# FFN norm of a hybrid decoder step: transposes by the DMA crossbar in place of TensorE and PSUM

## The chip, the cores and the metric

One Trainium2 chip, all eight cores, batch split over the cores, one launch. The metric is the device time of the slowest core in microseconds (us). Some executions fall in a second, slower state, in which the cores of a die run at a lower granted TensorE clock (in one run on record, of before_held, 1143.48 us with one die at clocks of 0.80 to 0.83, where fast runs of the same kernel took 1017 to 1026 us at 0.95 to 0.97). A run is also called slow when it is over 1.5% above the fastest of its kernel. Medians below are of all runs of a kernel, slow ones too.

## The reference

One layer: an RMS norm, one wide input projection, two groups of mixer heads (a gMLP and an mLSTM), an output projection with residual; then the part that the change touches, an RMS norm and a squared-ReLU MLP; then a gated per-layer embedding (PLE).

```python
D_MODEL = 1024; BATCH = 8; SEQ = 2048; DEC_BATCH = 128; DEC_SEQ = 8; D_FF = 4 * D_MODEL
def _layer(h, pe, state, ...):
    ...                                           # mixer: norm, projections, gMLP, mLSTM with carried state C, n, m
    h = h + jnp.concatenate([y_gm, y_ml], axis=-1) @ w_out
    # channel mixer: squared-ReLU MLP
    f = rmsnorm(h, norm_ffn) @ w_up
    h = h + jnp.square(jax.nn.relu(f)) @ w_down
    # per-layer input embedding
    gate = jax.nn.sigmoid(rmsnorm(h, norm_ple) @ w_ple_gate)
    h = h + gate * (pe @ w_ple_proj)
    return h, state, vg
```

Per core this is one prompt sequence of 2048 tokens (16 tiles of 128) and 16 sample sequences of 8 tokens (one more tile). The samples carry an mLSTM state, `state_C` (`sC` below), which is loaded from memory.

## The kernel before

The 17 tiles run in two super-groups: first eight prompt tiles and the sample tile, then eight prompt tiles. Each goes through a mixer stage (A), an MLP stage (B) and a PLE stage (C). The MLP streams its weights in four quarters, and takes tiles in groups of three. At the end of each mixer stage there is a *hand-over*, where the FFN norm of the first tiles must be done before TensorE can begin on the MLP. The change acts at the two hand-overs, nine tiles at the first, eight at the second.

The norm of a tile, with its transposes:

```python
def norm_T(g, so, hsrc, abf, dst, goff, junk=None):
    ss, rs, tmp = small(g, so, 1), small(g, so + 1, 1), small(g, so + 2, 1)
    act(abf if junk is None else junk, hsrc, AF.Square, accum=ss)      # ScalarE; its by-product goes into abf too
    rstd(rs, tmp, ss, 1.0 / DM, EPS)                                   # GpSimd
    o_ = act(abf, hsrc, AF.Copy, scale=rs)                             # ScalarE: fp32 -> bf16
    p = psb("N")                                                       # one PSUM bank
    trs([(p[:, kc * 128:(kc + 1) * 128], abf[:, kc * 128:(kc + 1) * 128], IDB[:]) for kc in range(8)])   # TensorE
    tt("dve", dst, p.rearrange("p (k t) -> p k t", k=8),
       GN[:, goff:goff + 8].unsqueeze(2).to_broadcast([128, 8, 128]), ALU.mult)   # VectorE: the gain
    return o_
```

The MLP stage around it. `AB` has two buffers; the weight loads, which cast fp32 to bf16, go through GpSimd's queue (q0 below):

```python
def load_q(qd):                                   # one quarter of w_up and of w_down
    ...
    for hf in range(2):
        dma(wu[:, :, hf * 512:(hf + 1) * 512], w_up_v[:, :, c0:c0 + 512], eng="pool")
    for hf in range(2):
        dma(wd[:, hf * 4:(hf + 1) * 4, :], w_down[r0:r0 + 512, :].rearrange("(f p) n -> p f n", p=128), eng="pool")
...
load_q(0)
for i, t in enumerate(sg):
    sl = t["slot"]
    norm_T(sl, 44, H[:, sl, :], AB[i % 2], A2T[sl // 3][:, :, sl % 3 * 128:(sl % 3 + 1) * 128], G_FFN)
load_q(1)
tgs = [sg[0:3], sg[3:6], sg[6:]]
for qd in range(4):
    for tg in tgs:
        ffn_group(qd, tg)                         # 64 matmuls of 128x384, then 48 of 128x512
        ...                                       # stage C after the last quarter
    ...
    if qd == 1:
        dma(WG, w_pg.rearrange("(k p) n -> p k n", p=128), eng="pool")   # PLE weights
        ...
    if qd + 2 < 4:
        load_q(qd + 2)
```

At the end of the last mixer tile the prompt state is stored, through SyncE's queue:

```python
if t["i"] == NPT - 1:
    for h in range(4):
        dma(o_Cp[h], CST[:, h, 0:128])                                                        # 4 x 64 KB
    dma(o_Np.rearrange("h d -> d h"), CST[:, :, 128], allow_slow_non_contiguous=True)         # 2 KB
    dma(o_Mp.rearrange("a h -> h a"), MPREV[:, 0:1], allow_slow_non_contiguous=True)
```

None of this is run in the order written. A list scheduler puts the operations of each engine in a fixed order at build time, from a model of their cost. In that model all DMAs, whoever issues them, share one pipe:

```python
if o.dma:
    free[e] = s + o.cost
    d0 = max(free[e] + 1.0, dma_free)
    dma_free = d0 + o.nbytes / 290e3
    o.fin = dma_free + 1.2
```

## Time and profile before

The median of the first three runs is 1023.42 us (1022.73 to 1027.23). The profiled execution spans 1020.3 us on its slowest core, core 2; the eight cores span 1003.6 to 1020.3 us, at granted clocks of 0.950 to 0.959.

| reading | before |
|---|---|
| TensorE busy | 895.8 us, 88% |
| chain that ended last | 75% TensorE, 9% DMA, 6% VectorE |
| TensorE busy in the first hand-over, 190-235 us | 23.5 of 45 us |
| TensorE busy in the middle of the second MLP, 760-935 us | 174.3 of 175 us |

All operations are emitted by one helper, so all have line L252 (DMA issues L276). One reads by the names of the tiles: `AR` is the big SBUF arena, `pb` a PSUM bank, `IDB` the identity, `GN` the gains, `H` the residual. The page of before, from its parts on busy time, queues, chain and groups (a group gives: operation and shape, count | busy us, mean ns of one | idle us of the engine just before them, what ended most of it):

```profile
PE 895.8 (88%) x5807; PEld 539.0 (53%) x5875; DVE 581.2 (57%) x1118; ACT 391.8 (38%) x711; POOL 264.4 (26%) x370
...
q0 software_dynamic: 54224, 59.18, 40.9%
q1 hardware_dynamic: 26380, 30.32, 9.8%
...
PE 75%; DMA 9%; DVE 6%; issue 5%; ACT 3%; POOL 2%; DVEq 0%; SPq 0%; POOLq 0%; ACTq 0%
...
L252 PE MATMUL pb<-AR 128*128 128x512 bf16 (+4 forms) x4856 | 838.0, 331 | 62.3 <-DVE AR L252 20.9
...
L252 ACT ACTIVATE AR<-H 128x1024 bf16<-128x1024 f32 x68 | 71.7, 1054 | 54.4 <-PE pb L252 26.9
L252 PE MATMUL pb<-IDB,AR 128*128 128x128 bf16 x578 | 53.5, 237 | 42.6 <-ACT AR L252 28.7
...
L252 DVE TENSOR_TENSOR AR<-pb,GN 128x1024 bf16<-128x1024 bf16 x51 | 61.6, 1218 | 36.4 <-PE pb L252 36.4
```

Two DMA queues: q0, the weights, and q1, which holds everything that SyncE issues (packets, MB, share of 16 engines' span). The `IDB` group holds all the transposes; 136 of the 578 belong to the FFN norm. The multiply by a gain takes 1.22 us.

The waits of TensorE in before (what it waited for: total us, times, longest):

```profile
PE pb L252 <- DVE AR L252: 29.6, 31, 3.2
PE pb L252 <- DMA AR<-sC: 15.7, 1, 15.7
```

TensorE in time order in before (start us, us, operation, count, [idle before it <- what ended it]), around the first and the second hand-over:

```profile
218.80 1.03 PE L252 MATMUL pb<-AR 128*128 128x129 bf16 x8 [15.66 <-DMA AR<-sC]
...
232.10 2.05 PE L252 MATMUL pb<-IDB,AR 128*128 128x128 bf16 x16 [3.81 <-ACT AR L252]
234.69 4.59 PE L252 MATMUL pb<-AR 128*128 128x384 bf16 x16 [0.54 <-DVE AR L252]
...
725.94 3.21 PE L252 MATMUL pb<-AR 128*128 128x384 bf16 x24 [0.31 <-DVE AR L252]
```

Three things are to be seen. Sixteen transposes, two tiles' worth, take 2.05 us. The first up-projections of the MLP, `128x384`, start almost without a wait. And they start while the mixer is not finished: after 234.69 and after 725.94 mixer matmuls still follow, so the MLP fills the mixer's gaps. The large wait at the first hand-over is for the sample state, `sC`.

The windows of before (stretch, then length and busy us of PE, PEld, DVE, ACT and POOL with counts, then granted clock, DMA share, GB/s):

```profile
195.00:270.00 75.00, 48.20 (x330) 30.85 (x332) 39.56 (x86) 25.26 (x49) 24.42 (x33) 0.77 0.80 112
760.00:935.00 175.00, 174.32 (x1009) 98.77 (x1018) 74.86 (x127) 38.75 (x81) 8.06 (x12) 1.00 0.49 79
```

### The profile page before, as it was taken

What the parts mean: (1) busy time and instruction counts of PE and PEld (TensorE: products, weight loads), DVE (VectorE), ACT (ScalarE), POOL (GpSimd) and SP (SyncE); (2) the same over time, 40 slices, a digit from 0 to 9 for tenths busy, and PEclk for the clock granted to TensorE, in tenths of its full rate; (3) what the DMA queues carried; (4) which work ended last, traced back from release to release, by engine and by line L of the source; (5) the groups of instructions that cost most, each with busy time, mean ns of one, the idle gap of its engine ahead of it and who ended that gap; (6) DMA issues with size and microseconds to landing.
All of it is one profiled execution on the core that took longest, in us unless ns stands there. A gap on an engine that the chain in (4) does not pass through costs nothing.

```text
span 1020.3 us, 17111 instructions; the slowest of 8 cores (1003.6 to 1020.3 us)
## 1 busy us (share of the span) xinstructions
PE 895.8 (88%) x5807; PEld 539.0 (53%) x5875; DVE 581.2 (57%) x1118; ACT 391.8 (38%) x711; POOL 264.4 (26%) x370
## 2 busy tenths in 40 slices
PE   2578898937999999999997678998899999999994
PEld 2465476624455555555553267576656555565542
DVE  2354878445656774444665537988864444445664
ACT  4245356425311121114544547655532112124543
POOL 3233345443202220011232323545520001001211
PEclk9798899967999999999999889999999999999997
DMA  9993010996677768065249400003999909000111
GB/s 166 183 172 45 12 45 6 109 146 97 104 142 136 177 161 133 1 86 88 86 105 203 121 22 2 1 2 51 138 144 162 161 2 155 11 1 4 68 45 62
DMA packets 80689, 90.59 MB, mean 89 GB/s; under 512 B 13656, under 2 KB 62044, under 8 KB 80604
## 3 DMA queue, kind: packets, MB, share of 16 engines
q0 software_dynamic: 54224, 59.18, 40.9%
q1 hardware_dynamic: 26380, 30.32, 9.8%
q8 instruction: 48, 0.79, 0.3%
q14 instruction: 37, 0.30, 0.1%
HBM read 134.74 MB, written 13.93 MB: 146 GB/s over the span
## 4 chain that ended last, share of the span: by engine, by line
PE 75%; DMA 9%; DVE 6%; issue 5%; ACT 3%; POOL 2%; DVEq 0%; SPq 0%; POOLq 0%; ACTq 0%
PE pb L252 75%; DVE AR L252 3%; DMA AR<-sC 3%; DMA AR<-w_in 3%; DMA AR<-pp 2%; ACT AR L252 2%; POOL SMALL L252 1%; DMA H<-xp 1%; DVE H L252 1%; DVE SMALL L252 1%; DVE ROWX L252 1%; ACT L252 1%; POOL AR L252 0%; DVE ROWR L252 0%; POOL CST L252 0%
## 5 line engine op out<-in xcount | busy, mean ns | idle before, releaser
L252 PE MATMUL pb<-AR 128*128 128x512 bf16 (+4 forms) x4856 | 838.0, 331 | 62.3 <-DVE AR L252 20.9
L252 PEld LDWEIGHTS pb<-AR 128*128 128x128 bf16 x4924 | 470.8, 100 | 393.8 <-issue 86.3
L252 ACT ACTIVATE AR<-pb 128x384 f32<-128x384 f32 (+5 forms) x349 | 175.5, 513 | 476.0 <-PE pb L252 387.7
L252 DVE TENSOR_TENSOR H<-H,pb 128x512 f32<-128x512 f32 x170 | 116.4, 685 | 136.5 <-PE pb L252 136.3
L252 DVE TENSOR_TENSOR AR<-AR 128x384 bf16<-128x384 f32 (+2 forms) x209 | 122.8, 589 | 109.1 <-ACT AR L252 108.3
L252 ACT ACTIVATE AR<-H 128x1024 bf16<-128x1024 f32 x68 | 71.7, 1054 | 54.4 <-PE pb L252 26.9
L252 PE MATMUL pb<-IDB,AR 128*128 128x128 bf16 x578 | 53.5, 237 | 42.6 <-ACT AR L252 28.7
L252 POOL TENSOR_SCALAR SMALL<-SMALL 128x1 f32<-128x1 f32 x85 | 26.3, 310 | 245.4 <-ACT AR L252 201.9
L252 DVE TENSOR_TENSOR AR<-pb,GN 128x1024 bf16<-128x1024 bf16 x51 | 61.6, 1218 | 36.4 <-PE pb L252 36.4
L252 POOL TENSOR_TENSOR SMALL<-SMALL,NEGH 128x1 f32<-128x1 f32 (+1 forms) x102 | 69.3, 681 | 49.8 <-DVE SMALL L252 29.6
L252 PEld LDWEIGHTS pb<-IDB,AR 128*128 128x128 bf16 x578 | 43.0, 107 | 57.7 <-issue 48.9
L252 ACT ACTIVATE AR<-H,SMALL 128x1024 bf16<-128x1024 f32 x51 | 58.1, 1145 | 35.3 <-POOL SMALL L252 34.9
L276 POOL DMA_DIRECT2D AR<-w_up x16 | 15.0, 935 | 132.7 <-PE pb L252 132.3
L252 DVE TENSOR_TENSOR AR<-pb,AR 128x512 f32<-128x512 f32 (+3 forms) x86 | 43.7, 523 | 9.4 <-ACT AR L252 8.4
L252 ACT ACT_TABLE_LOAD x29 | 37.2, 1283 | 16.1 <-PE pb L252 10.2
L252 DVE SCALAR_TENSOR_TENSOR AR<-AR,pb 128x512 f32<-128x512 f32 x34 | 23.2, 684 | 29.6 <-PE pb L252 20.8
L252 ACT ACTIVATE AR<-AR 128x512 f32<-128x512 f32 x34 | 21.3, 629 | 23.8 <-DVE AR L252 17.2
L252 POOL TENSOR_TENSOR AR<-AR,GROW 128x512 bf16<-128x512 f32 (+1 forms) x19 | 25.5, 1341 | 16.5 <-PE pb L252 8.5
L276 POOL DMA_DIRECT2D AR<-w_in x12 | 11.0, 920 | 68.3 <-PE pb L252 64.3
L252 DVE SCALAR_TENSOR_TENSOR AR<-H,SMALL,AR 128x1024 f32<-128x1024 f32 x17 | 22.9, 1346 | 9.1 <-POOL SMALL L252 8.7
L252 ACT ACTIVATE AR<-pb,GSM 128x129 f32<-128x129 f32 x68 | 20.7, 366 | 13.7 <-PE pb L252 13.5
L276 POOL DMA_DIRECT2D AR<-w_down x16 | 12.2, 765 | 51.4 <-PE pb L252 51.3
(101 smaller groups left out, 434.7 us busy)
## 6 DMA issues: line engine op xcount, KB each, us to landing
AR<-w_up POOLq DMA_DIRECT2D x16, 1024.0 KB, 16.0
AR<-w_down POOLq DMA_DIRECT2D x16, 1024.0 KB, 18.9
AR<-w_in POOLq DMA_DIRECT2D x12, 1024.0 KB, 17.5
H<-xp SPq DMA_DIRECT2D x16, 512.0 KB, 4.6
y_p<-AR SPq DMA_DIRECT2D x16, 512.0 KB, 2.9
AR<-w_out POOLq DMA_DIRECT2D x2, 2048.0 KB, 41.8
AR<-sC SPq DMA_DIRECT2D x8, 512.0 KB, 5.0
AR<-w_pg POOLq DMA_DIRECT2D x2, 2048.0 KB, 27.4
```

Source lines behind the costliest of these rows:

```text
L252: ins = getattr(e, name)(**kw)
L276: lambda e, out=out, in_=in_, sem=sem, kw=kw: e.dma_start(out=out, in_=in_, **kw).then_inc(sem, 16))
```

## The change

The intent is to take the FFN norm's transposes off TensorE, the busiest engine, and to free a PSUM bank: SyncE issues one transposing DMA per tile (128x1024 bf16, 256 KB, SBUF to SBUF), and VectorE then multiplies in place.

```diff
+        def dma_t(out, in_):
+            nb = 2 * _nelem(out) * 128
+            return P.add("sp", (out, in_, dict(transpose=True)), [in_], [out], 0.06, dma=True, nbytes=nb)
+
-        def norm_T(g, so, hsrc, abf, dst, goff, junk=None):
+        def norm_T(g, so, hsrc, abf, dst, goff, junk=None, xbar=False):
             ss, rs, tmp = small(g, so, 1), small(g, so + 1, 1), small(g, so + 2, 1)
             act(abf if junk is None else junk, hsrc, AF.Square, accum=ss)
             rstd(rs, tmp, ss, 1.0 / DM, EPS)
             o_ = act(abf, hsrc, AF.Copy, scale=rs)
+            if xbar:
+                dma_t(dst, abf)
+                tt("dve", dst, dst, GN[:, goff:goff + 8].unsqueeze(2).to_broadcast([128, 8, 128]), ALU.mult)
+                return o_
             p = psb("N")
@@ stage B
-                norm_T(sl, 44, H[:, sl, :], AB[i % 2], A2T[sl // 3][...], G_FFN)
+                norm_T(sl, 44, H[:, sl, :], AB[i % 2], A2T[sl // 3][...], G_FFN, xbar=True)
```

The other two norms keep their TensorE transposes.

More of the change, by code (lines that the diff above doesn't have):

```diff
@@ L1222, in build @@
                 sl = t["slot"]
-                norm_T(sl, 44, H[:, sl, :], AB[i % 2], A2T[sl // 3][:, :, sl % 3 * 128:(sl % 3 + 1) * 128], G_FFN)
+                norm_T(sl, 44, H[:, sl, :], AB[i % 2], A2T[sl // 3][:, :, sl % 3 * 128:(sl % 3 + 1) * 128], G_FFN, xbar=True)
             load_q(1)
```

## The prediction

> **What bounds the kernel now.** TensorE. The page gives PE 88% busy and 75% of the chain that ended last. In the middle of the MLP it is packed: the window view gives PE 174.3 of 175 us at 760-935. It is not where the mixer hands over to the MLP: PE 23.5 of 45 us at 190-235, 56.3 of 60 at 700-760. The change acts only there (nine tiles, then eight).
>
> **What goes.** Per tile eight 128x128 PE transposes and one PSUM bank. The PE timeline shows 16 of them in 2.05 us, so about 1.0 us per tile, 17 us in all. That bounds the gain.
>
> **What stays.** The VectorE gain multiply (1.22 us from PSUM). It now reads bf16 from SBUF[...]: I expect 1.1-1.25 us.
>
> **What comes.** 17 SyncE DMAs of 256 KB, SBUF to SBUF. [...] the trace of before has none of the first, and its TensorE transposes take about 130 ns each, pipelined. [...] weights load at the hand-overs. DMA share is about 1.1 at 190-240 and at 705-780. There SyncE's own DMAs of 64-512 KB took 8 to 20 us to land (64 KB state stores 9.1-14.3, a 512 KB load 19.9), against 3.7 us for 512 KB in a quiet stretch. Estimate for a transpose: 4-5 us quiet, 10-18 us (central 13) beside weight loads.
>
> **Critical path.** Two AB buffers feed the transposes. TensorE let AB go within 1 us; now it is held until the DMA lands, and the square of tile i+2 writes into AB too. So tiles go in pairs: landing + about 4-5 us (square 1.24, rstd on POOL 1.3, scale 1.15, twice over ScalarE). The first MLP group needs tiles 0-2, so two rounds. The static order also moves: the first up-projection goes behind all, or most, of the last mixer stage, where before it filled that stage's gaps.
>
> - Second hand-over: before starts the first group at 725.9 and has it done at 757.6. After: norms of tiles 2 and 3 stand behind the mixer's ScalarE work, about 738; transposes issue about 742, land about 755, multiply, group starts about 757 and needs 22 us of PE: done about 779. Loss about 21 us, of which about 8 is not the DMA.
> - First hand-over: two transposes can run in the 15.7 us wait for the state load, but they share its DMA. Group start 234.7 -> about 247, partly paid back by mixer work done earlier and by absent transposes: loss about 4 us.
> - Idle TensorE restarts at a low clock (granted 0.50 at 210-220 in the window view): 1-2 us.
>
> Later groups have 22 us of PE work to hide two tiles' transposes; that holds below about 17 us of landing.
>
> **Time.** 1023.4 + about 25 = **1048 us**, 8 in 10 within 1025-1078. Faster by over 2%: 0.03; within 2%: 0.40; slower by over 2%: 0.57.
>
> **What shows it.** PE busy down 15-18 us, yet a longer span; new idle of TensorE before the 128x384 matmuls at both hand-overs, ended by the VectorE multiply behind a DMA; transposes landing in 10 us or more at the second; the multiply near 1.2 us; squares on ScalarE waiting on a DMA; the rest of the MLP unchanged.
>
> **What would make it wrong.** Landings near 4 us even beside weight loads: then about +10 us. Transposes that crowd out weight loads, or land after 20 us: 1070 and more. Mixer stage ending sooner without interleaved MLP work: a smaller loss.

"The first" are transposes by DMA, and the two landing estimates are from the landings of before that stand in front of them. The sum came to 21 + 4 = 25 us on top of 1023.4 (the 1-2 us for the clock stand outside it). The low clock of an idle TensorE is in the traces: in before 0.50 was granted in 210-220 us, where TensorE was busy for 1.2 of 10 us, and 1.00 in 240-250; in after it was 0.50 in 806-809 us, right behind a hole of 35.3 us, and 1.00 in 810-815.

## The result, and the profile after

The result is correct. The median is 1095.38 us (1093.41 to 1098.69, 4 runs) against 1024.8 us for before in the same rounds: ratio 1.0691, 95% interval 1.0651 to 1.0731, slower. Ratios here and below are the mean time of one kernel's fast runs over that of the other's of the same rounds, so not quite the ratio of the medians that are quoted. The direction was predicted. The size was not: +71 us against +25.

The page of after, the lines that answer to those of before:

```profile
PE 902.1 (83%) x5739; PEld 534.0 (49%) x5739; DVE 587.1 (54%) x1118; ACT 392.2 (36%) x711; POOL 269.1 (25%) x370
...
q0 software_dynamic: 54224, 59.18, 40.7%
q1 hardware_dynamic: 44332, 34.78, 13.8%
...
PE 65%; DMA 20%; DVE 5%; issue 4%; ACT 3%; POOL 2%; SPq 1%; DVEq 0%; POOLq 0%; ACTq 0%
...
L252 PE MATMUL pb<-AR 128*128 128x512 bf16 (+4 forms) x4924 | 852.7, 334 | 131.9 <-DVE AR L252 64.5
...
L252 ACT ACTIVATE AR<-H 128x1024 bf16<-128x1024 f32 x68 | 71.7, 1055 | 99.2 <-DMA AR<-AR 61.7
...
L252 PE MATMUL pb<-IDB,AR 128*128 128x128 bf16 x442 | 42.8, 238 | 38.1 <-ACT AR L252 25.7
...
L252 DVE TENSOR_TENSOR AR<-AR,GN 128x1024 bf16<-128x1024 bf16 x17 | 20.4, 1219 | 49.9 <-DMA AR<-AR 49.9
```

The transposes left TensorE as intended: 136 fewer, 10.7 us less busy. The in-place multiply takes 1219 ns, the same as from PSUM. The hardware queue has 17,952 more packets, which is 1,056 for each of 17 transposes, for only 4.46 MB. DMA's share of the chain rose from 9% to 20%.

The waits of TensorE in after:

```profile
PE pb L252 <- DVE AR L252: 70.7, 28, 35.3
PE pb L252 <- DMA AR<-sC: 46.9, 4, 21.7
```

TensorE in time order in after, around the two hand-overs (core 7, the slowest):

```profile
222.62 1.02 PE L252 MATMUL pb<-AR 128*128 128x129 bf16 x8 [21.74 <-DMA AR<-sC]
...
228.77 1.03 PE L252 MATMUL pb<-AR 128*128 128x129 bf16 x8 [4.70 <-DMA AR<-sC]
...
250.28 1.03 PE L252 MATMUL pb<-AR 128*128 128x129 bf16 x8 [15.88 <-DMA AR<-sC]
255.85 1.89 PE L252 MATMUL pb<-AR 128*128 128x129 bf16 x16 [4.54 <-DMA AR<-sC]
...
767.25 3.61 PE L252 MATMUL pb<-AR 128*128 128x512 bf16 x16 [1.05 <-DVE AR L252]
806.15 10.96 PE L252 MATMUL pb<-AR 128*128 128x384 bf16 x56 [35.29 <-DVE AR L252]
```

At the second hand-over one hole of 35.3 us stands before the first up-projection. It is put down to VectorE, whose multiply came last; VectorE itself was waiting for a transpose. At the first hand-over there is no such hole. TensorE instead waits four times for the *sample state*, 46.9 us in place of 15.7: these are mixer matmuls, and no MLP work stands in the static order that could fill their gaps.

The chain of after beside the hole (start us, us, what): the transpose of tile 2, which took SyncE 10.5 us to issue, and that of tile 3, which took 36 us to land. TensorE's hole ends at 806.15, when tile 2 is there; the chain goes on to 817, since ScalarE's square of a later tile waits for the buffer that tile 3 still holds:

```profile
770.32 10.47 SPq L276
780.95 36.21 DMA AR<-AR
```

SyncE's queue in time order in after, second hand-over:

```profile
743.30 11.66 SPq L276 DMA_TRANSPOSE AR<-AR  x2
756.89 2.13 SPq L276 DMA_DIRECT2D o_Cp<-CST  x4
759.11 0.39 SPq L276 DMA_DIRECT2D o_Np<-CST  x1
770.32 30.39 SPq L276 DMA_TRANSPOSE AR<-AR  x2
```

One transpose at a time, from issue to landing: 16.3 and 21.3 us for tiles 0 and 1, 34.4 and 36.2 us for tiles 2 and 3, which were queued behind the five state stores. The last of the stage, after the weights had landed, took 3.2 to 3.3 us each.

The DMA view of after for 794-803 us, while weights and the transposes of tiles 2 and 3 were both in flight (packets, MB, share of 16 engines):

```profile
q0 software_dynamic: 814, 1.60, 95.2%
q1 hardware_dynamic: 816, 0.20, 17.5%
```

In these slices, where both queues had work, they moved packet for packet: 814 of the weights' (about 2 KB), 816 of the transposes' (256 B). The same in finer slices: 276 to 276 in 794-797 us, 274 to 277 in 797-800, 464 to 465 in 761-764. These counts are what one gets if a small packet waits for a large one at every turn. A weight packet took about 95 ns in the records at 1 KB (761-764 us) and about 165 to 175 ns at 2 KB (794-803 us). A transpose has 1,024 packets of 256 B (4,096 for the four in 818-835 us). If they are spread evenly over the 16 engines, that is 64 each, so beside 2 KB packets our estimate is 64 x 0.17 = 11 us, and about 22 us for a pair in one queue. The first pair fits that: the first was issued at 743.3, and the two landed at 759.6 and 766.4.

The windows of after, which answer to those of before:

```profile
195.00:270.00 75.00, 23.12 (x154) 15.37 (x152) 27.17 (x62) 19.86 (x38) 22.86 (x28) 0.59 1.27 123
740.00:826.00 86.00, 36.38 (x196) 18.62 (x195) 28.74 (x50) 20.11 (x41) 18.88 (x25) 0.68 1.02 134
826.00:1018.00 192.00, 191.98 (x1102) 106.88 (x1101) 87.98 (x143) 48.77 (x99) 12.41 (x21) 1.00 0.33 48
```

TensorE did 48.2 us of work in 195-270 us before, and 23.1 after. Once the second MLP runs, nothing differs.

To sum the losses, four intervals were taken from the trace of every core, as medians over the eight cores of one profiled execution:

- to the first store of a finished tile (it holds the first hand-over and all of the first MLP);
- the second mixer stage, from there to the last gate matmul of its last group;
- the second hand-over: from that gate matmul to the 256th up-projection (`128x384`) of the second MLP;
- the rest, from there to the end.

| median over cores, us | before | after | difference |
|---|---|---|---|
| to the first store of a finished tile | 482.1 | 511.0 | +28.9 |
| second mixer stage, up to its last gate matmul | 229.0 | 227.5 | -1.5 |
| second hand-over | 105.2 | 156.3 | +51.1 |
| the rest | 192.3 | 191.4 | -0.9 |
| span | 1008.5 | 1087.7 | +79.2 |

The median cores differ by 79 us, the slowest cores (which give the time) by 72, because the spans of before are spread more widely. The intervals tell where, not the exact sum.

### The profile page after: what moved, and what is told of

It reads as the page before. It is cut to its first block, busy times and chain, and to the rows that moved or that the text cites. A ratio compares the mean times of both kernels' runs of the same rounds, so it can differ in the third digit from the quotient of the medians.

```text
span 1092.5 us, 16916 instructions; the slowest of 8 cores (1071.1 to 1092.5 us)
## 1 busy us (share of the span) xinstructions
PE 902.1 (83%) x5739; PEld 534.0 (49%) x5739; DVE 587.1 (54%) x1118; ACT 392.2 (36%) x711; POOL 269.1 (25%) x370
## 4 chain that ended last, share of the span: by engine, by line
PE 65%; DMA 20%; DVE 5%; issue 4%; ACT 3%; POOL 2%; SPq 1%; DVEq 0%; POOLq 0%; ACTq 0%
PE pb L252 65%; DMA AR<-sC 9%; DMA AR<-w_in 4%; DMA AR<-AR 3%; DVE AR L252 3%; ACT AR L252 2%; DMA AR<-pp 2%; DMA H<-xp 1%; POOL SMALL L252 1%; SPq L276 1%; DVE H L252 1%; POOL AR L252 0%; POOL AR L276 0%; DVE SMALL L252 0%; POOL CST L252 0%
## 5 line engine op out<-in xcount | busy, mean ns | idle before, releaser
L252 PE MATMUL pb<-AR 128*128 128x512 bf16 (+4 forms) x4924 | 852.7, 334 | 131.9 <-DVE AR L252 64.5
L252 DVE TENSOR_TENSOR AR<-AR 128x384 bf16<-128x384 f32 (+2 forms) x209 | 127.9, 615 | 100.0 <-ACT AR L252 98.7
L252 ACT ACTIVATE AR<-H 128x1024 bf16<-128x1024 f32 x68 | 71.7, 1055 | 99.2 <-DMA AR<-AR 61.7
L252 POOL TENSOR_TENSOR SMALL<-SMALL,NEGH 128x1 f32<-128x1 f32 (+1 forms) x102 | 71.5, 702 | 42.1 <-DVE SMALL L252 20.3
L252 PE MATMUL pb<-IDB,AR 128*128 128x128 bf16 x442 | 42.8, 238 | 38.1 <-ACT AR L252 25.7
L252 PEld LDWEIGHTS pb<-IDB,AR 128*128 128x128 bf16 x442 | 33.7, 108 | 51.2 <-issue 44.1
L252 DVE TENSOR_TENSOR AR<-pb,GN 128x1024 bf16<-128x1024 bf16 x34 | 41.2, 1219 | 30.6 <-PE pb L252 30.6
L252 DVE TENSOR_TENSOR AR<-AR,GN 128x1024 bf16<-128x1024 bf16 x17 | 20.4, 1219 | 49.9 <-DMA AR<-AR 49.9
L252 DVE SCALAR_TENSOR_TENSOR AR<-AR,pb 128x512 f32<-128x512 f32 x34 | 23.1, 684 | 29.4 <-PE pb L252 22.6
L252 ACT ACTIVATE AR<-AR 128x512 f32<-128x512 f32 x34 | 21.3, 630 | 33.4 <-DVE AR L252 26.5
L252 POOL TENSOR_TENSOR AR<-KTOKS,SEQ 128x1024 bf16<-128x1024 bf16 x8 | 15.2, 1901 | 60.0 <-PE pb L252 59.9
```

The costliest lines, as they stand in the source:

```text
L252: ins = getattr(e, name)(**kw)
```

## The experiments

Theory: the transposes land late because their packets take turns with the weight packets and stand in one queue behind each other and behind SyncE's stores; TensorE waits for that, and two `AB` buffers pair the tiles. Rivals: (a) only the static order matters, since the scheduler's model puts a transpose behind the weight loads, and so puts MLP work after the mixer; (b) the traffic slows the weights and the state, and TensorE waits for those.

Traces show whether an edit moved the static order. In stores_late and np_late every compute engine's order is that of after, and in traffic_only and before_stores_late that of before. order_only has after's order with 136 transposes put in on TensorE. In the other seven the order moved as well, since the scheduler sees the edit.

All outputs are right.

### Only the traffic: before, with transposes that nobody waits for

```diff
+ o_ = norm_T(...)                                   # TensorE transposes, as before
+ if si == 1:                                        # second hand-over
+     P.add("sp", (XD[i % 2], WGT[:].rearrange("p k n -> p (k n)"), dict(transpose=True)), [WGT[:]],
+           [XD[i % 2]], 0.06, dma=True, after=[o_])
```

Eight transposes of the same size from the resident weight tile `WGT` into scratch; the model is told that they cost no DMA time, so every other engine keeps its order.

> The kernel before, untouched in order on TensorE, VectorE, ScalarE and GpSimd, plus eight DMA transposes of the same size at the second hand-over that nobody's arithmetic waits for (a constant weight tile into a scratch area that is overwritten later). Theory Wait: the changed kernel loses because work waits for the landings, not because the 2 MB of extra traffic slow other loads; within 4 us of before, about 1025. Theory Contention: the extra packets delay the MLP weights enough to stall TensorE; 8 us or more over before. The landings of the dummies should be 10-35 us either way.

Measured: 1028.66 us (1014.13 to 1033.88), ratio 0.9993 (0.993 to 1.0056): same. This rests on two runs, 1014.13 and 1024.13. The other two, 1033.19 and 1033.88, count as slow because they are over 1.5% above the fastest, though no die had a lower clock; with all four the mean is 0.6% above before's. The trace, of one of these two, is the better witness: the landings were long (19.7 us in the median of the slowest core), and yet the median core took as long for the second hand-over, as defined above, as in before, within 0.1 us. So there the traffic alone costs nothing that can be seen, and rival (b) falls at this hand-over. What costs is to wait for a transpose.

### The state stores moved behind the transposes

```diff
-                    if t["i"] == NPT - 1:
-                        ...                          # o_Cp x4, o_Np, o_Mp stored at once
+            if si == 1:
+                store_state([nl])                    # the same stores, after the last norm of the stage
```

> The changed kernel, with only the final mLSTM state stores (four of 64 KB, and the 2 KB one that goes out in 4-byte pieces) issued after the last norm of the second hand-over instead of in its middle. TensorE's order is the same. Theory Q (queue): the transposes of tiles 2 and 3, which took 33-39 us to land there, stood in the SyncE queue behind the 4-byte stores; they should land in 12-18 us and the time fall by 14-22 us, to about 1077. Theory W (weights): the length comes from weight packets alone; the landings stay above 28 us and the time within 4 us of 1095.

Measured: 1077.79 us (1077.59 to 1096.41; the last is a slow run), ratio 1.0526 (1.0487 to 1.0565). The time fell by about 18 us, as expected, but the landing was not what was expected. The transpose of tile 3 came down from 36 to 46 us in after's cores to 27 to 29 us (those of tile 2 have no recorded landing here). TensorE in time order, second hand-over:

```profile
792.46 10.61 PE L252 MATMUL pb<-AR 128*128 128x384 bf16 x56 [21.16 <-DVE AR L252]
```

The hole on TensorE fell from 35.3 to 21.2 us. The stores were about two fifths of it; the rest is taken up below.

The control, the same move in before, where no transpose stands behind the stores:

> Control: the kernel before with the same state stores issued after the last norm; TensorE, VectorE, ScalarE and GpSimd orders identical. Both theories: nothing on the critical path waits for these stores in before, so within 3 us of before. If it were faster by over 5 us, part of stores_late's gain would have nothing to do with transposes.

Measured: 1024.73 us, ratio 1.0008 (0.9977 to 1.0039): same. The stores themselves cost before nothing. They matter because of what is queued behind them.

### The 2 KB store alone

```diff
-                        dma(o_Np.rearrange("h d -> d h"), CST[:, :, 128], allow_slow_non_contiguous=True)
...
+            if si == 1:
+                dma(o_Np.rearrange("h d -> d h"), CST[:, :, 128], allow_slow_non_contiguous=True, after=[nl])
```

The four 64 KB stores stay in front. Every other engine's order is identical to after's, in the traces too.

> The changed kernel with one DMA moved in the SyncE queue and every other engine's order identical: the 2 KB store that goes out as 512 pieces of 4 bytes is issued after the transposes instead of just ahead of those of tiles 2 and 3. Theory N: these pieces, each of which takes its turn with a weight packet like any other, are what the two transposes stood behind; 12-18 us of stores_late's 17, so about 1080. Rival: the four 64 KB stores ahead of it (512 pieces of 512 bytes) are as much to blame, each piece costing the same turn; half or less of the gain, 1086 or more.

Measured: 1076.39 us (1074.03 to 1080.26), ratio 1.0524 (1.0484 to 1.0565), as good as with all the stores moved; so the four 64 KB stores, the rival, cost next to nothing. TensorE in time order, second hand-over:

```profile
787.19 12.09 PE L252 MATMUL pb<-AR 128*128 128x384 bf16 x56 [21.53 <-DVE AR L252]
```

The store of 2 KB costs 17 us by the ratios and 19 by the medians. It is written in 512 pieces of 4 bytes. The DMA view of after for 773-791 us:

```profile
q0 software_dynamic: 469, 0.96, 87.0%
q1 hardware_dynamic: 451, 0.02, 4.8%
```

The two queues again moved alike, 469 packets of the weights' and 451 of SyncE's, of which 366 are 4-byte pieces. In that stretch the weight packets themselves took far longer than elsewhere: 0.53 us in the mean, and up to 1.2 us in the mean of a 3-us slice, against 0.17 us beside the transposes. The count of turns alone would not explain the cost: at 0.17 us a turn our estimate for 512 pieces over 16 engines is 32 x 0.17 = 5.4 us. Most of the 17 to 19 us comes with the longer turns, and why they are longer is left open.

### The order alone: after's order, transposes by TensorE

```diff
+        pos = {o.idx: i for i, o in enumerate(order)}  # after the scheduler has run on the changed program
+        ...                                            # find a PSUM bank that is free from some place on until the multiply
+            for d, m, b in put.get(o.idx, ()):
+                E.op("pe", [("transpose", dict(out=PBB[b][...], in_=src[...], identity=IDB[:])) for kc in range(8)], ...)
+            if o.__dict__.get("skip_"):                # the transposing DMA is not emitted
+                continue
```

> The instruction order of the changed kernel on every engine, but the nine and eight transposes done by TensorE into a PSUM bank that is free at that place: no DMA transposes. Theory O (order): the static order, which puts the first MLP group behind the mixer stage, costs by itself; 10-20 us over before, about 1038, most of it at the first hand-over, where the waits for the state loads are no longer filled. Theory L (landing): nearly all of the loss is waiting for the landing; within 5 us of before, about 1025.

Measured: 1055.15 us, ratio 1.0282 (1.0231 to 1.0333); one of four runs, at 1110.21, was slow and is not in the ratio. The expectation, 1038, was too low: by the ratio the order, with the transposes on TensorE, costs about 29 us. The waits of TensorE in this kernel:

```profile
PE pb L252 <- DVE AR L252: 38.6, 33, 3.6
PE pb L252 <- DMA AR<-sC: 28.4, 4, 14.2
```

The hole before the MLP is gone (the longest wait for VectorE is 3.6 us), but TensorE still waits four times for the sample state, as in after, where before it waited once. By intervals: to the first store 496.9 us, 14.8 above before; second hand-over 122.7, 17.5 above. So of after's +28.9 and +51.1 us, about 15 and 17 belong to the order. At the second hand-over this is an upper bound, as the next run shows: here the transposes still stand in TensorE's own order. Rival (a) is right for up to about 40% of the loss, and wrong for the rest.

### No weights beside the second hand-over

The stores late, as above, and the loads of the second weight quarter and of the PLE weights held until the last norm of the second super-group:

```diff
+            if si == 1:
+                store_state([nl])
+            af = [nl] if si == 1 else []
-            load_q(1)
+            load_q(1, after=af)
-                    dma(WG, w_pg.rearrange("(k p) n -> p k n", p=128), eng="pool")
+                    dma(WG, w_pg.rearrange("(k p) n -> p k n", p=128), eng="pool", after=af)
```

> As stores_late, and at the second hand-over the weights of the second MLP quarter and the PLE weights are held back until the last norm is done, so that only the first quarter's weights, which are needed at once, share the DMA engines. Theory W (weights share the engines packet for packet): from the third transpose on, landings fall to 3-6 us, the first pair stays at 11-17 us; about 30 us less than the changed kernel, about 1063. Theory Q: nothing beyond what stores_late gave, about 1077. If the held-back weights come too late for the second quarter, some is lost again there.

Measured: 1055.5 us (1050.18 to 1065.92; one of four runs, 1056.08, counts as slow), ratio 1.0323 (1.025 to 1.0397), less than the 1063 that was expected. The DMA view of this kernel for 735-860 us (operation, count, median us to landing):

```profile
AR<-AR SPq DMA_TRANSPOSE x8, 3.1
```

With nothing beside them the transposes land in 3.1 us. (The first pair, which still met the end of the first quarter's weights, has no recorded landing.) The second hand-over takes 110.6 us, 5.4 above before and even below the 122.7 of the order alone. The order is not a fixed price: in the scheduler's model too the transposes no longer stand behind the held weights, and in the trace 16 up-projections now come before the mixer's last 16 matmuls. In order_only, besides, TensorE has to do the transposes in its own order. How the 12 us divide between the two is not tested. The first hand-over is untouched (510.4 us to the first store, after had 511.0), and that is what the kernel still loses.

### The first hand-over: the state before the transposes

```diff
-            return P.add("sp", (out, in_, dict(transpose=True)), [in_], [out], 0.06, dma=True, nbytes=nb)
+            return P.add("sp", (out, in_, dict(transpose=True)), [in_], [out], 0.06, dma=True, nbytes=nb, after=csl[-2:])
```

`csl` holds the loads of the sample state that the mixer waits for; a transpose waits for the last two of them.

> The changed kernel, with the first transposes held (first hand-over only) until the last two loads of the sample state have landed. Theory S: there the transposes take packets from the state loads, for which TensorE waits: last of them 55 us after the last input projection, 41 us in order_only. Held back, they should be at about 41 again, the first MLP group no later, and the time 6-13 us under the changed kernel, about 1086. Rival: the state loads are slow anyway and the transposes' own lateness counts; the first group starts later by about as much as the hold, and the time is the same or worse.

Measured: 1098.51 us, ratio 1.0769 (1.0747 to 1.0791): no gain, where 1086 was expected. The state did come sooner (the hold also moved TensorE's order at this hand-over, so not by the packets alone): its last load landed at 234.7 us (median over cores) against 252.3 in after and 237.5 in before. The first MLP group could then start earlier. But the transposes that had been pushed back met the next weight loads: on core 5 the later ones took 20.5 and 31.4 us, and the second group waited for them. To the first store it took 514.6 us. The loss was moved, not removed.

### A better model of the transpose for the scheduler

```diff
-            if o.dma:
+            if o.dma and "transpose" in o.calls[2]:
+                free[e] = s + o.cost
+                o.fin = free[e] + 3.2               # the quiet landing, outside the weights' pipe
+            elif o.dma:
```

> The changed kernel, with one line of the scheduler's model changed: a transpose is taken to land in 3.2 us (what a lone one took on the chip) and no longer to queue behind the weights. At the first hand-over this puts seven of the first group's up-projections back before the sample tile's last state product; at the second it changes little. Theory O (order can be mended by itself): 8-15 us under the changed kernel, about 1083. Rival L: TensorE now waits in order for the landing in the middle of the mixer; within 5 us of 1095, or slower.

Measured: 1110.66 us (1110.23 to 1111.24), ratio 1.0891 (1.0871 to 1.0911), slower than after. TensorE in time order in this kernel, first hand-over:

```profile
248.40 11.59 PE L252 MATMUL pb<-AR 128*128 128x384 bf16 x74 [14.22 <-DVE AR L252]
```

The scheduler now puts MLP matmuls among the mixer's, as in before, and TensorE, which keeps to that order in the trace, stands before them for 14.2 us with mixer work behind it. The landings really took 11.6 us at this hand-over and 18.1 us at the second (medians of those recorded on the slowest core), where the model had 3.2. With such landings the pessimistic order of after is the better one (1095.38 us against 1110.66).

### Everything held, at both hand-overs

State first, the stores late, and the second weight quarter and PLE weights held at both hand-overs (the edits above together, with `af = [nl]`).

> All the cures together on the changed kernel: state loads first, state stores late, second-quarter and PLE weights held until the norms are done, at both hand-overs. If the causes found so far (order, stores in the queue, weights and state loads sharing the engines) are the whole of it, the landings are 3-7 us except the second hand-over's first pair, the second hand-over costs under 10 us as in both_late, the first about what order_only lost (15 us): about 1042. If over 1055, a cause is missing.

Measured: 1021.83 us (five runs, one of them, 1150.71, slow), ratio 1.0022 (0.9991 to 1.0054): the same as before, better than the 1042 that was expected. TensorE in time order in this kernel, the hand-overs' longest waits:

```profile
231.63 1.03 PE L252 MATMUL pb<-AR 128*128 128x129 bf16 x8 [8.79 <-DMA AR<-sC]
...
740.88 2.72 PE L252 MATMUL pb<-AR 128*128 128x384 bf16 x8 [7.08 <-DVE AR L252]
```

No loss can be seen in the time any more. The transposes of the first hand-over land in 3.1 to 3.4 us, where a landing is recorded. By intervals, it took 478.0 us to the first store (before 482.1), and 115.0 in the second hand-over (before 105.2; its first pair still meets the first quarter's weights). The order moved with the landing: at the first hand-over TensorE now has 100 of the mixer's `128x256` matmuls between two of its waits for the state. So `held` shows that the loss can be undone, not how much of that is the landing. In the control, before with the same holds for weights and stores:

> Control for held: the kernel before, TensorE transposes kept, with the same holds (second-quarter and PLE weights after the norms at both hand-overs, state stores late). If holding weights helps by itself, because the sample state loads no longer queue behind two second-quarter weight loads, the last state load comes some 8 us earlier and this beats before by 3-10 us, about 1016, and then the crossbar itself is still a loss of 5 us or so against its own fair rival. If held owed its recovery to the crossbar alone, this stays within 2 us of before.

Measured: a median of 1023.47 us over 8 runs of which three were slow; the five fast ones give a ratio of 0.9971 (0.9939 to 1.0003): same. The last state load came 9 us earlier (228.4 us in the median core, before 237.5), as expected, and the interval leaves room for a gain of up to 6 us. So the crossbar has not bought anything in `held`: it came back to parity with before, and its ratio is 0.5% above that of this control, which has the same holds (the two were not run in the same rounds, so this difference is not shown).

Held without the state-first wait:

> held without the hold for the state loads. If the first transposes do take their packets from the state loads, the last of these comes 5-13 us later and the time is about 1030; if holding the weights is what counts, it is within 3 us of held, about 1022.

Measured: 1035.58 us (five runs, one of them, 1117.49, slow), ratio 1.0097 (1.0058 to 1.0136); the mean of the fast runs is 1033, near the 1030 that was expected. The last state load landed at 239.4 us, against 224.4 in `held`, and the first store came at 490.4, against 478.0. So the transposes in front of the state go with about 12 us of time at the first hand-over even when no second weight quarter is there. This pair is not a clean one, since TensorE's order at this hand-over differs between the two. The clean pair is after and order_only, with the same order: there the last state load comes 12.8 us later with the transposing DMAs (252.3 against 239.5), and the first store 14.1 us later. At this hand-over, for the state loads, rival (b) holds.

### Only the tiles that are not needed first

All of `held`, with the 3.2 us model, but tiles 0 to 2 of each stage transposed by TensorE (`xbar=sl >= 3`).

> held, but the transposes of the first MLP group (tiles 0 to 2 of each hand-over) stay on TensorE and only tiles 3 and later go through the crossbar, where 22 us of matmuls can hide their landing. The model takes a transpose to land in 3.2 us. If the landing is harmless where there is work to hide it, this keeps about 11 us of TensorE time and loses nothing at the start of the group: 8-14 us under before, about 1012, the fastest so far. If the AB buffers or the order still bite, within 3 us of before or slower.

Measured: 1032.63 us (1027.58 to 1034.04), ratio 1.0085 (1.006 to 1.0111): under 2%, but clearly not the 1012 that was expected. Against `before_held`, which was run in the same rounds, it is 1.1% slower (1031.4 and 1019.7 us, means of the fast runs). Eleven tiles' transposes, 88 matmuls, left TensorE, and on the slowest core the others landed in 3.1 to 5.1 us. The busy time shows little of it: over the six cores of each kernel whose matmul records are complete, the medians are 894.3 us and 896.6 in the control. (The slowest core's 892.8 us lacks 68 records and must not be compared.) Nothing of it became time. TensorE waits 2.2 us for a held `w_up` at the second quarter, and both intervals are about 3 us longer than the control's (484.4 against 481.6 us, 108.8 against 106.0); why is open. No version with the crossbar beat before.

What the pairing of tiles over two buffers costs by itself is open.

## Why the prediction was right or wrong

**Right.** Slower. TensorE bounds the kernel and the change acts at two hand-overs. The transposes go in pairs (743.3, 770.3, 819.6 us). The transposes are gone from TensorE. The multiply is the same, 1219 ns where 1.1 to 1.25 us was predicted. A quiet landing takes 3.1 to 3.3 us (4 to 5 predicted). The `128x384` matmuls at the second hand-over are idle behind VectorE, behind a DMA (at the first, where this was predicted too, they are not: the waits there are for the sample state). ScalarE's squares wait for a DMA (61.7 us). The middle of the MLP is unchanged.

**Wrong: "PE busy down 15-18 us".** The transposes' group fell by 10.7 us, and total busy rose from 895.8 to 902.1. These totals cannot be compared: the trace of before's slowest core lacks records of 68 matmuls (4856 `pb<-AR` matmuls for 4924 weight loads). Over the six cores of each kernel with complete records the medians are 898.3 and 895.8 us, 2.5 us less. That the lower mean clock (0.950 before, 0.914 after on the slowest cores) takes the rest is not shown. The group would have been the better witness to name.

**Wrong: the landing, "10-18 us (central 13) beside weight loads".** This is the term that was most mis-sized at the second hand-over. It was taken from single plain DMAs of before, by bytes, as if a transpose shared the engines and nothing else. That the two queues shared them fits the trace (814 and 816 packets); the step from there to a duration was wrong in two ways. First, it is packets that took turns: 814 against 816. If 1,024 small packets wait for as many large ones, a pair in one queue takes about 22 us by our estimate (23.1 measured), not 13. Second, what else stood in that queue was not looked at: five stores at 756.9 to 759.5 us, one of them in 512 pieces. Tiles 2 and 3 took 34 and 36 us. Of the 51 us at this hand-over, going by intervals, 17 are the order (122.7 - 105.2), 17 the 4-byte store (156.3 - 139.4, the interval of the run with that store moved), and 17 the landing beside the weights (139.4 - 122.7). The split in three is an estimate: the run with the order alone still has the transposes on TensorE, so the order's part is too large and the landing's too small by some us (with the weights held the whole hand-over cost 5.4 us).

**Wrong: the order, "about 8 is not the DMA".** It is up to 17 at the second hand-over, and about 15 at the first, where none was counted. The prediction saw that up-projections would go behind the mixer, but booked mixer work done earlier as a repayment. Measured, the mixer then waits for its own inputs, the sample state, with nothing to fill in.

**Wrong: the first hand-over, "loss about 4 us".** It is 29. The step that failed reads "two transposes can run in the 15.7 us wait for the state load". That wait was no free slot: the wait *was* a DMA, and the transposes took turns with it. In after, in 210-225 us, GpSimd's queue, with the state loads in it, moved 1,444 packets (1,249 of them 256-byte pieces) and SyncE's, with the first two transposes, 1,440. The last two state loads are issued only when TensorE has used the earlier ones (224.2 and 230.4 us), so the delay is handed on. The last state load landed at 252.3 us where the same order without transposing DMAs had it at 239.5. About 15 us are order (496.9 - 482.1), about 14 the rest (511.0 - 496.9), and in two pairs of kernels the state's delay is seen: 12.8 us here, and 15.0 in `held_no_state` against `held`, where the first store came 12.4 us later (there the order moved too).

The sum of the predicted losses, 4 + 21, became 29 + 51 in the median core. The list of what would make the prediction wrong did name the case ("land after 20 us: 1070 and more"), and gave it too little weight.

## What to carry to other kernels

Moving work from the bound engine to a DMA lost here where the landing was waited for: it was 16 to 36 us for the first four of the second hand-over in place of 3.1 to 3.3 us quiet, and the kernel took 1095.38 us in place of 1024.8. Cost such a landing by the packets that take turns with it (814 to 816 here) and by everything ahead of it in its queue (17 to 19 us for one 2 KB store here), not by its bytes and a bandwidth. An engine's wait for a DMA need not be free time for another DMA: here the transposes delayed the last state load by 13 us. And in a statically ordered kernel a later landing, or a model that believes in one, also moves the work that used to fill the gaps (order_only, ratio 1.0282): run the new order without the new operation to see that price by itself.

## What the traces show of a transposing DMA

- Beside weight loads the records of the two queues came one for one (814 to 816 in 794-803 us, 276 to 276 in 794-797), of 256 B against 2 KB. By the estimate above, the *number* of small pieces, and how long each turn is, make up the landing there (64 x 0.17 = 11 us for one, 22 for a pair). A 256 KB transpose, 3.1 to 3.3 us quiet, took up to 36 us on the slowest core.
- A store in tiny pieces delayed what was queued behind it: 2 KB in 512 pieces of 4 bytes cost the kernel 17 to 19 us. In before, where no transpose is queued behind it, moving it with the other state stores changed nothing (ratio 1.0008).
- A transpose took SyncE 1.2 us to issue in a quiet stretch, and up to 19.8 us on the slowest core while earlier DMAs of its queue were in flight; what SyncE issued next waited too (800.87 us, right behind those 19.8).
- Eight 128x128 in one DMA landed in 3.1 to 3.3 us; TensorE's took about 130 ns each in a row (16 in 2.05 us). No run here shows one alone by DMA.
- 256 KB transposed landed in 3.1 to 3.3 us quiet. Regular DMAs landed in 2.6 us (a load of the same 256 KB, `wsT`, with nothing beside it, at 113.2 us in after), and at twice the size in 3.7 us (a load) and 2.6 us (stores of finished tiles) in before.
